# A retention and RWKV-7 decoder trunk: small matmuls in four quarters of the array, a written order table, and the first three projections summed side by side

## The chip, the cores and the metric

The program runs on one core of a Trainium2 chip. The metric is the device time of one execution in microseconds (us), lower is better. A core has five engines that run their own instruction streams: PE (TensorE, matmuls, with its weight loads listed apart as PEld), DVE (VectorE), ACT (ScalarE), POOL (GpSimd) and SP (SyncE, which here only issues DMAs). PE writes its sums into PSUM, which has eight banks; DVE and ACT read them out.

## The reference, cut to what matters

Two residual layers of width 1024 over 1024 tokens, a SwiGLU feed-forward net behind each, and a final norm. Everything that the change touches lies in the mixer of layer 0:

```python
z = h @ w_in                                  # 1024 x 3840
z_ret, z_rwkv = z[..., :4 * RET_WIDTH], z[..., 4 * RET_WIDTH:]
...                                           # 8 retention heads from z_ret
zs = z_rwkv + mu * (token_shift(z_rwkv) - z_rwkv)
rr, kr, vr, wl, al, gl = jnp.split(zs, split_at, axis=-1)
...                                           # decay, a, gate, kk from the low-rank parts
def step(state, inp):                         # 8 RWKV heads of 64, token by token
    r_t, w_t, k_t, v_t, a_t, b_t = inp
    sa = jnp.einsum('bhij,bhj->bhi', state, a_t)
    state = state * w_t[:, :, None, :] + sa[..., None] * b_t[:, :, None, :] + v_t[..., None] * k_t[:, :, None, :]
    return state, jnp.einsum('bhij,bhj->bhi', state, r_t)
...
return jnp.concatenate([ret_out, rwkv_out], axis=-1) @ w_out
```

## The kernel before, in words

Activations are kept transposed, features on the partitions and tokens along the free side, in two halves of 512 tokens (`HT`). A big product is made of float32r matmuls of 128 x 128 weights on 128 x 512 activations; each factor is split into a rounded high part and the rest, so that one product takes three matmuls (high by high, high by low, low by high) and one output tile of 128 features 24 of them. `wsplit` makes the split of a weight tile: a cast on ACT (L339) and a subtraction on DVE or POOL (L340).

The mixer (`mixer0`) has 60 such projections: for each half the two low-rank ones (`lora`), twelve for r, k, v of the RWKV heads and sixteen for the retention heads. They are `jobs` of the class `Plan`. Each sums into one of three PSUM banks of the tag "f" and is then read out by its `evac`, which multiplies by the row factor `self.rs` of the norm (L638 for the RWKV parts, through a single buffer `z`).

Between them stand the small matmuls of the heads, in plain float32, which the profile shows as two records each. They sum into four banks of the tag "m" and one of the tag "c". The RWKV heads go in pairs: partitions 0 to 63 hold one head, 64 to 127 the other. A generator `pair` prepares one pair of one half (eight in all, letters below are tile names):

- n: `BK` by `AR`, 16 matmuls of 64 rows by 64 columns of the array with 64 moving columns; read out by DVE (L726) into `DT` and sent by DMA to `dn`.
- GG: `BK` by `AR`, 64 rows by 128 columns; read out by DVE (L766).
- the transposes of `BK` and of v (`rv`), L258, and the copy of `AR` through an identity into `XA`.
- UV by GG, again 64 by 64, into the other half of `XA`.

A generator `unit` then works on two pairs (four units): it solves a 32 x 32 triangular system on DVE (`X`), fetches it by DMA into `GT`, completes `GT` through two groups of 32 x 32 matmuls (TZ), and runs GT by XA (64 by 64, 128 moving columns), GG by GG (the same shape), and then a chain of eight dependent steps over the chunks (GT, L950 on DVE) that carries the state. `ret` does the retention heads.

In the 64 by 64 groups the two heads of a pair use the array's quarters on the diagonal: rows 0 to 63 with columns 0 to 63, and rows 64 to 127 with columns 64 to 127.

The order is set in two stages. `Plan.run` keeps a clock of its own (`self.now`, advanced by a cost for each matmul) and decides from due times in the `yield`s which generator goes on and when the next third of a projection product is issued. What it emits is then put into each engine's queue by a list scheduler of the framework, which can move instructions a short way past each other.

At the start `loads` fetches the eight x tiles with the first two weight tiles (512 KB each) between them; `first_norm` multiplies x by the norm's gain (ACT L472, DVE L473), squares it (ACT L538) and adds (DVE L540); the sum over the features is a matmul with ones, and `factor` makes `self.rs` from it (L482, L483).

Behind the mixer come the output projection (`wout`, L354 to L356, whose first half is already fed in between the last unit's matmuls), the feed-forward net, the attention layer and its net. They are the same before and after.

Of the kernel before, what the change touches and what calls it, by code (L numbers as in the profile page):

```python
# [16 lines left out]
P = 128  # L17
T = 1024
HT = 512
# [5 lines left out]
CW = math.exp(-0.5)  # L25
NCH = 8
# [75 lines left out]

class Plan:

    def __init__(self, K):
        self.K, self.now, self.ev, self.banks = K, 0.0, {}, []
        self.gens, self.jobs, self.cur, self.twice = [], deque(), None, ()
        self.proj = None  # L110

    def chain(self, g):
        self.gens.append([g, (), self.now])
        return self

    def job(self, name, hf, col, rhs, evac, need=()):
        self.jobs.append(dict(name=name, hf=hf, col=col, rhs=rhs, evac=evac, need=need, raw=None, hl=None))

    def done(self, name):
        self.ev[name] = self.now  # L120

    def time(self, need, t):
        for n, d in need:
            if n not in self.ev:
                return None
            t = max(t, self.ev[n] + d)
        return t

    def rsok(self):
        return self.K.rs is not None  # L130

    def room(self):

        self.banks = [t for t in self.banks if t > self.now]
        return len(self.banks) < 3.0
# [13 lines left out]
    def busy(self):  # L149

        if self.cur is not None:
            return self.cur["k"] < len(self.cur["rhs"])
        if not self.jobs:
            return False
        t = self.time(self.jobs[0]["need"], 0.0)
        return t is not None and t <= self.now

    def step(self):
        c = self.cur
        if c is None:  # L160
            if not self.jobs:
                return None
            t = self.time(self.jobs[0]["need"], 0.0)
            if t is None or t > self.now:
                return t
            self.prefetch()
            c = self.cur = self.jobs.popleft()
            self.prefetch()
            c["ps"], c["k"], c["rhs"] = self.K.pst("f", [P, HT]), 0, c["rhs"]()
        k = c["k"]  # L170
        if k >= len(c["rhs"]):
            return None
        (hi, lo), (rh, rl) = c["hl"][k], c["rhs"][k]
        n = KT
        self.K.mm(c["ps"], hi, rh, start=k == 0, stop=False)
        self.K.mm(c["ps"], hi, rl, start=False, stop=False)
        self.K.mm(c["ps"], lo, rh, start=False, stop=k == n - 1)
        c["k"] += 1
        if c["k"] == n:
            c["evac"](c["ps"])  # L180
            self.done(c["name"])
            self.cur = None
        return self.now

    def run(self):
        while self.gens or self.jobs or self.cur:
            nxt = []
            hold = self.proj is not None and self.busy() and self.rsok() and self.now - self.proj < 0.0
            for g in self.gens:
                t = self.time(g[1], g[2])  # L190
                if not hold and t is not None and t <= self.now and (self.room() or not self.busy()):
                    self.proj = None
                    try:
                        need, d = next(g[0])
                        g[1], g[2] = need, self.now + d
                    except StopIteration:
                        self.gens.remove(g)
                    break
                if t is not None:
                    nxt.append(max(t, self.now + 0.1))  # L200
# [1806 lines left out]
```

## Time and profile before

| what | value |
|---|---|
| three runs | 2315.28, 2315.53, 2315.76 us, median 2315.53 |
| the profiled execution's own time | 2311.46 us |
| its span | 2308.4 us, granted PE clock 0.996 on the mean |
| PE busy | 2260.1 us, 98% of the span |
| DVE busy | 1606.3 us, 70% |
| ACT busy | 1040.5 us, 45% |
| first product matmul | 5.88 us |
| last mixer matmul | about 642 us |

The span is what the profiler saw of one execution; the execution's own time holds 3.06 us more. In the timeline a row stands for a run of like instructions: its start, its length to the end of the last one, how many, and in brackets the idle time of the engine before it. Since matmuls overlap, what a run costs PE is read from its start to the start of the next run, not from its length.

### The profile page before, as it was taken

What the parts mean: (1) busy time and instruction counts of PE and PEld (TensorE: products, weight loads), DVE (VectorE), ACT (ScalarE), POOL (GpSimd) and SP (SyncE); (2) the same over time, 40 slices, a digit from 0 to 9 for tenths busy, and PEclk for the clock granted to TensorE, in tenths of its full rate; (3) what the DMA queues carried; (4) which work ended last, traced back from release to release, by engine and by line L of the source; (5) the groups of instructions that cost most, each with busy time, mean ns of one, the idle gap of its engine ahead of it and who ended that gap; (6) DMA issues with size and microseconds to landing.
All of it is one profiled execution on the core that took longest, in us unless ns stands there. A gap on an engine that the chain in (4) does not pass through costs nothing.

```text
span 2308.4 us, 34970 instructions
## 1 busy us (share of the span) xinstructions
PE 2260.1 (98%) x12980; PEld 1799.4 (78%) x12980; DVE 1606.3 (70%) x2786; ACT 1040.5 (45%) x1962; POOL 432.3 (19%) x439
## 2 busy tenths in 40 slices
PE   8999999999999999999999999999999999999997
PEld 6777777777777888888888877677788888888885
DVE  6876865875567358887677538557448788878778
ACT  5454433414456334444333546456545444443334
POOL 3233221212551000000001743342331000000000
PEclk9999999999999999999999999999999999999998
DMA  8565644443445655663753422242336565647652
GB/s 290 196 226 185 196 145 139 130 126 110 146 174 183 211 176 200 210 215 128 263 215 135 135 84 67 64 137 81 110 132 233 187 215 201 213 179 286 237 203 103
DMA packets 168264, 396.19 MB, mean 172 GB/s; under 512 B 42912, under 2 KB 46112, under 8 KB 168096
## 3 DMA queue, kind: packets, MB, share of 16 engines
q1 hardware_dynamic: 164976, 388.41, 49.8%
q10 hardware_dynamic: 2832, 4.52, 0.5%
q8 instruction: 102, 1.67, 0.3%
q0 software_dynamic: 288, 1.05, 0.1%
q14 instruction: 66, 0.54, 0.1%
HBM read 271.62 MB, written 116.92 MB: 168 GB/s over the span
## 4 chain that ended last, share of the span: by engine, by line
PE 65%; DVE 4%; ACT 2%; issue 1%; DMA 1%; POOL 1%; SPq 0%; ACTq 0%; DVEq 0%; POOLq 0%
PE ps_m L1193 7%; PE ps_m L1192 7%; PE ps_m L1191 7%; PE ps_f L355 4%; PE ps_f L354 4%; PE ps_f L356 4%; PE ps_f L1191 4%; PE ps_f L1192 4%; PE ps_f L1193 4%; PE ps_c L1192 2%; PE ps_c L1193 2%; PE ps_c L1191 2%; PE ps_r L1193 2%; PE ps_r L1192 2%; PE ps_r L1191 2%; PE ps_rc L1674 1%
## 5 line engine op out<-in xcount | busy, mean ns | idle before, releaser
L247 PE MATMUL ps_f<-n,w 128*128 128x512 f32 x1440 | 374.4, 409 | 7.9 <-ACT w L339 5.9
L247 PEld LDWEIGHTS ps_f<-n,w 128*128 128x128 f32 x1440 | 266.8, 190 | 87.5 <-issue 18.6
L340 POOL TENSOR_TENSOR w<-wr,w 128x512 fp32r<-128x512 f32 (+1 forms) x130 | 178.8, 1382 | 383.4 <-ACT w L339 326.4
L339 ACT CAST w<-wr 128x512 fp32r<-128x512 f32 x240 | 145.8, 612 | 167.5 <-PE ps_f L356 65.6
L354 PE MATMUL ps_f<-n,w 128*128 128x512 f32 x356 | 140.6, 396 | 2.4 <-DVE h L603 1.6
L356 PE MATMUL ps_f<-n,w 128*128 128x512 f32 x356 | 140.7, 396 | 1.3 <-POOL w L340 1.3
L355 PE MATMUL ps_f<-n,w 128*128 128x512 f32 x356 | 141.2, 397 | 0.3 <-POOL n L362 0.3
L1191 PE MATMUL ps_f<-n,w 128*128 128x512 f32 x322 | 126.7, 395 | 2.3 <-ACT u L1345 1.6
L1192 PE MATMUL ps_f<-n,w 128*128 128x512 f32 x322 | 125.7, 391 | 0.0
L1193 PE MATMUL ps_f<-n,w 128*128 128x512 f32 x322 | 124.5, 392 | 0.0
L340 DVE TENSOR_TENSOR w<-wr,w 128x512 fp32r<-128x512 f32 x110 | 81.3, 740 | 44.3 <-ACT w L339 44.1
L1191 PE MATMUL ps_m<-n,w 128*128 128x512 f32 x282 | 109.7, 389 | 0.0
L1192 PE MATMUL ps_m<-n,w 128*128 128x512 f32 x282 | 109.7, 389 | 0.0
L1193 PE MATMUL ps_m<-n,w 128*128 128x512 f32 x282 | 109.5, 389 | 0.0
L1191 PE MATMUL ps_m<-cb,w 128*128 128x512 f32 x240 | 93.4, 389 | 0.0
L1192 PE MATMUL ps_m<-cb,w 128*128 128x512 f32 x240 | 93.4, 389 | 0.0
L1193 PE MATMUL ps_m<-cb,w 128*128 128x512 f32 x240 | 93.4, 389 | 0.0
L362 POOL TENSOR_TENSOR ha<-hr,ha 128x512 fp32r<-128x512 f32 x4 | 5.9, 1470 | 447.5 <-ACT ha L360 446.8
L340 DVE TENSOR_TENSOR w<-wq,w 128x512 fp32r<-128x512 f32 x92 | 63.5, 691 | 33.1 <-ACT w L339 32.6
L354 PEld LDWEIGHTS ps_f<-n,w 128*128 128x128 f32 x356 | 66.8, 188 | 19.4 <-issue 2.0
L355 PEld LDWEIGHTS ps_f<-n,w 128*128 128x128 f32 x356 | 66.8, 188 | 18.9 <-issue 4.8
L339 ACT CAST w<-wq 128x512 fp32r<-128x512 f32 x92 | 57.2, 622 | 53.2 <-PE ps_m L1193 29.5
(529 smaller groups left out, 5887.3 us busy)
## 6 DMA issues: line engine op xcount, KB each, us to landing
hc<-n SPq DMA_DIRECT2D x74, 512.0 KB, 3.1
wsp<-w SPq DMA_DIRECT2D x54, 512.0 KB, 3.0
w<-wsp SPq DMA_DIRECT2D x54, 512.0 KB, 3.6
wq<-in_w_gate SPq DMA_DIRECT2D x44, 512.0 KB, 4.1
u<-u SPq DMA_DIRECT2D x88, 256.0 KB, 3.0
n<-hc SPq DMA_DIRECT2D x43, 512.0 KB, 6.4
hid<-n SPq DMA_DIRECT2D x66, 256.0 KB, 2.1
ha<-hc SPq DMA_DIRECT2D x33, 512.0 KB, 5.8
```

The costliest lines, as they stand in the source:

```text
L247: i = self.nc.tensor.matmul(out, lhsT, rhs, **kw)
L339: nc.scalar.copy(hi[:, :n], raw[:, c])
L340: (lo or self.lo).tensor_tensor(out=l[:, :n], in0=raw[:, c], in1=hi.bitcast(F32)[:, :n], op=ALU.subtract)
L354: nc.tensor.matmul(ps, hi, rh, start=k == 0, stop=False)
L355: nc.tensor.matmul(ps, hi, rl, start=False, stop=False)
L356: nc.tensor.matmul(ps, lo, rh, start=False, stop=k == n - 1)
L362: e.tensor_tensor(out=lo, in0=src, in1=hi.bitcast(F32), op=ALU.subtract)
L1191: mm(ps, hi, xh, start=first and k == 0, stop=False, skip_group_check=True)
L1192: mm(ps, hi, xl, start=False, stop=False, skip_group_check=True)
L1193: mm(ps, lo, xh, start=False, stop=last and k == len(w) - 1, skip_group_check=True)
L1674: nc.tensor.matmul(ps[:, e, i, kw], qt[2 * g + i][a, P * b : P * b + P], src[a, P * b + P * k0 : P * b + 256], start=True, stop=True,)
```

## The change

- **Four quarters.** In the 64 by 64 groups (n, the copy of AR, UV by GG, GT by XA, GG by GG) some chunks now use the diagonal quarters as before and the others the two quarters off the diagonal, by the tables `XOF`, `YOF` and `ZOF`. The results of the off-diagonal quarters land on the partitions of the other head, so the order of the heads in `GG`, `XA`, `UV` and `M` changes with the chunk. Matmuls of different rows go to different banks: a group that took one bank takes two, and its read-out becomes two instructions of half the width.
- The transposes of `BK` alternate between the row halves. Those of v are cut in two: 64 rows and 64 moving columns where there were 128 and 128.
- The off-diagonal 32 x 32 blocks that the first TZ group reads now come by DMA through a new buffer `df`: two more writes for each pair and four more reads for each unit.
- **The order table.** `Plan`'s clock and due times are gone. A string `ORDER` says which generator goes on (a letter) and how many products of a projection are issued ahead of it (a number).
- **The start.** The first three projections are summed side by side in the three "f" banks, one feature tile after the other, from weight pieces (`w_first`, 128 x 384, laid out ahead by the host) that land in the places of the `BK` tiles. The next two sum into "m" banks. Six matmuls on a zeroed tile stand ahead of it all.

```diff
+XOF = [c // 2 % 2 for c in range(8)]
+YOF = [c % 2 for c in range(8)]
+ZOF = [c // 2 % 2 ^ c % 2 for c in range(8)]
+XS = (slice(0, 2), slice(2, 4))
+ZS = (slice(0, 4, 3), slice(1, 3))
...
+ORDER = (
+    "aabcdefghijklmnopqrstuv17f13f2g15f3f3g7f4f1f1f4gn2gf3f1f1n1bn3bg1nb1fgg1bg1g3bgng2b3b3b3b1g1b3b2ob3b3b1o1bo3"
...
+        for x in ORDER:
+            if x.isdigit():
+                n += x
+                continue
+            for _ in range(int(n or 0)):
+                self.step()
+            n = ""
+            next(self.gens[ord(x) - ord("a")], None)
...
+        ps = self.t(self.ps, [P, HT], "ps_c", 1)
+        for _ in range(6):
+            nc.tensor.matmul(ps[:, :200], self.idle[:, :P], self.idle, start=True, stop=True)
...
         for k in range(KT):
+            if k % 4 == 0:
+                raw = self.t(self.mz, [P, NCH, 3, 64], "BK", 2).rearrange("p a b c -> p (a b c)")
+            w = raw[:, k % 4 * 3 * P : (k % 4 + 1) * 3 * P]
             x = self.t(rp, [P, HT], "r2", 8)
+            self.keep(nc.sync.dma_start(w, self.A["w_first"][k]))
             self.keep(nc.sync.dma_start(x, self.A["xT"][k, :, 0:HT]))
...
+            j["bank"] = "m"
...
         for k in range(KT):
+            W.append(self.wsplit(wf[k], 3 * P))
+            self.nT.append(self.gained(x0[k], "n1a", n8, k))
...
+            for j, i in ((0, k), (1, k), (2, k - 1)):
+                if i >= 0:
+                    prods(j, i)
...
-        ps = self.pst("m", [P, NCH, 64])
-        for c in range(NCH):
-            for rs in half:
-                self.mm(ps[rs, c, :], BK[rs, c, 0, :], AR[rs, c, 0:64], start=True, stop=True)
+        pss = [self.pst("m", [P, 4, 64]) for _ in range(2)]
+        for c in (0, 2, 1, 3, 4, 6, 5, 7):
+            x = XOF[c]
+            for e, rs in enumerate(half):
+                self.mm(pss[x][half[e ^ x], c // 4 * 2 + c % 2, :], BK[rs, c, 0, :], AR[rs, c, 0:64], start=True, stop=True)
...
+        for q in range(2):
+            nc.sync.dma_start(
+                self.dfs[u][((p % 2) * 2 + q) * 8 : ((p % 2) * 2 + q) * 8 + 8].rearrange("c s t -> s c t"),
+                nd[64 * q : 64 * q + 32, :, 32:64],
+            )
...
-        for e in range(2):
-            ps = self.pst("m", [P, NCH, 64])
-            rs = half[e]
-            for c in range(NCH):
-                self.tr(ps[:, c, :], BK[rs, c, e : e + 2, :].rearrange("p a t -> p (a t)"), ident[rs, rs])
-            S.copy(GG[:, :, e, P:], ps)
+        pss = [self.pst("m", [P, NCH, 64]) for _ in range(2)]
+        for c in range(NCH):
+            for f in range(2):
+                e = f ^ YOF[c]
+                self.tr(pss[f][:, c, :], BK[half[f], c, e : e + 2, :].rearrange("p a t -> p (a t)"), ident[half[f], half[f]])
+        for f in range(2):
+            S.copy(G4[:, :, ZS[f], P:], pairs2(pss[f]))
...
+            for c in range(NCH):
                 for e, a in enumerate(half):
+                    self.mm(pss[ZOF[c]][half[e ^ ZOF[c]], c // 2, :], GT[a, c, :], XA[a, c, :], start=True, stop=True)
+            for f in range(2):
+                for e, a in enumerate(half):
+                    S.copy(four(GG[a, :, e, 0:64])[:, :, ZS[f], :], pairs2(pss[f][a, :, 0:64]))
+                    V.tensor_copy(four(UV[a, :, e, :])[:, :, ZS[f], :], pairs2(pss[f][a, :, 64:P]))
```

How PE's queue changes is seen at three places. In these rows the names are the bank that is summed into, then what streams through and what stands as weights; shape is that of the output. The first place is PE at the start of the program, where `n` and `w` are the split activations and weights. Before, one sum and then a second:

```order
L247 MATMUL ps_f_223<-n_37_166,w_114 128x512
L247 MATMUL ps_f_273<-n_35_164,w_127 128x512
L247 MATMUL ps_f_273<-n_39_168,w_127 128x512
L247 MATMUL ps_f_223<-n_41_170,w_114 128x512
L247 MATMUL ps_f_223<-n_37_166,w_114 128x512 x2
L247 MATMUL ps_f_273<-n_35_164,w_127 128x512 x2
L247 MATMUL ps_f_273<-n_39_168,w_127 128x512
```

And now, at the end of the three sums, with the matmul on ones for the norm and the fourth sum in an "m" bank:

```order
L215 MATMUL ps_f_171<-n_34_165,w_288 128x512
L215 MATMUL ps_f_172<-n_34_165,w_271 128x512
L215 MATMUL ps_f_172<-n_38_169,w_271 128x512
L215 MATMUL ps_f_172<-n_34_165,w_271 128x512
L215 MATMUL ps_m_313<-nq_293,c_ones_68 128x512
L215 MATMUL ps_f_172<-n_34_165,w_288 128x512
L215 MATMUL ps_f_172<-n_38_169,w_288 128x512
L215 MATMUL ps_f_172<-n_34_165,w_288 128x512
L1172 MATMUL ps_m_373<-n_31_162,w_305 128x512
```

The matmul on ones stood behind 59 product matmuls and now stands behind 69, and the sum that follows the first three no longer takes one of their banks. The second place is PE in the first pair of heads, the transposes of `BK`, the copy of `AR` and the transposes of v (`rv`), between products of the projections. Before:

```order
L258 MATMUL ps_m_807<-c_ident_154,BK_530 128x64 x8
L247 MATMUL ps_f_837<-n_39_168,w_732 128x512
L247 MATMUL ps_f_837<-n_35_164,w_732 128x512
L247 MATMUL ps_f_837<-n_36_165,w_732 128x512
L258 MATMUL ps_m_817<-c_ident_154,BK_530 128x64 x8
L247 MATMUL ps_m_842<-c_ident_154,AR_527 64x64 x16
L258 MATMUL ps_m_861<-c_ident_154,rv_424 128x128 x4
L247 MATMUL ps_m_874<-AR_701,BK_704 64x64 x16
L258 MATMUL ps_m_896<-c_ident_154,rv_424 128x128 x4
```

Now the same pair's transposes of `BK`, and further on the next pair's n:

```order
L218 MATMUL ps_m_844<-c_ident_152,BK_546 128x64 x6
L218 MATMUL ps_m_845<-c_ident_152,BK_546 128x64 x6
L218 MATMUL ps_m_844<-c_ident_152,BK_546 128x64
L218 MATMUL ps_m_845<-c_ident_152,BK_546 128x64
...
L215 MATMUL ps_m_876<-AR_724,BK_727 64x64 x2
L215 MATMUL ps_m_877<-AR_724,BK_727 64x64 x2
L215 MATMUL ps_m_876<-AR_724,BK_727 64x64 x2
L215 MATMUL ps_m_877<-AR_724,BK_727 64x64 x2
```

The n group alternates between two banks, that is between the quarters on and off the diagonal, by twos. The transposes do so only in part: the scheduler has put six of one row half ahead of six of the other. The third place is PE in the first unit, GT by XA. Before, four banks one after the other:

```order
L247 MATMUL ps_f_1814<-n_35_164,w_1647 128x512
L247 MATMUL ps_m_1739<-XA_841,GT_1459 64x128 x8
L247 MATMUL ps_m_1752<-XA_841,GT_1459 64x128 x8
L247 MATMUL ps_m_1765<-XA_1130,GT_1460 64x128 x8
L247 MATMUL ps_m_1778<-XA_1130,GT_1460 64x128 x8
```

Now two banks in turn, and then the other two:

```order
L215 MATMUL ps_m_1844<-XA_937,GT_1546 64x128 x2
L215 MATMUL ps_m_1845<-XA_937,GT_1546 64x128 x4
L215 MATMUL ps_m_1844<-XA_937,GT_1546 64x128 x4
L215 MATMUL ps_m_1845<-XA_937,GT_1546 64x128 x4
L215 MATMUL ps_m_1844<-XA_937,GT_1546 64x128 x2
L215 MATMUL ps_m_1870<-XA_1184,GT_1547 64x128 x2
L215 MATMUL ps_m_1871<-XA_1184,GT_1547 64x128 x4
```

The number of matmuls is the same; each bank now holds one set of quarters.

More of the change, by code (lines that the diff above doesn't have):

```diff
@@ L147, in prefetch @@
                     j["hl"] = self.K.wkept(kept) if j["hf"] else self.K.wsplit(j["raw"], keep=kept)
[L149 to L156, printed above, removed]
-    def step(self):
[L159 to L165, printed above, removed]
+    def step(self):
+        if self.cur is None:
             self.prefetch()
@@ L168, in step @@
             self.prefetch()
[L169 removed]
+            c["ps"], c["k"], c["rhs"] = self.K.pst(c.get("bank", "f"), [P, HT]), 0, c["rhs"]()
+        c = self.cur
         k = c["k"]
[L171 to L177, printed above, removed]
+        self.K.prod(c["ps"], [c["hl"][k]], [c["rhs"][k]], k == 0, k == KT - 1)
         c["k"] += 1
[L179 removed]
+        if c["k"] == KT:
             c["evac"](c["ps"])
[L181 removed]
             self.cur = None
[L183 removed]
     def run(self):
[L186 to L200, printed above, removed]
[L201 to L208 removed]
+        n = ""
[5 more added lines that the diff above has]
+                self.step()
+            n = ""
+            next(self.gens[ord(x) - ord("a")], None)
+        for _ in range(int(n or 0)):
+            self.step()
+        assert not self.jobs and self.cur is None
 class Kern:
@@ L297, in pst @@
     def pst(self, tag, shape):
-        if tag == "m" and self.plan:
-            self.plan.banks.append(self.plan.now + 3.0)
         return self.t(self.ps, shape, "ps_" + tag, self.psb[tag])
@@ new lines, in pair @@
+        for f in range(2):
+            S.copy(G4[:, :, ZS[f], P:], pairs2(pss[f]))
+        yield
+        XA = self.t(mp, [P, NCH, P], "XA", 2)
+        pss = [self.pst("m", [P, 4, 64]) for _ in range(2)]
+        for c in (0, 2, 1, 3, 4, 6, 5, 7):
+            x = XOF[c]
+            for e, rs in enumerate(half):
+                self.mm(
+                    pss[x][half[e ^ x], c // 4 * 2 + c % 2, :], AR[rs, c, 0:64], ident[rs, rs], start=True, stop=True
+                )
+        for f in range(2):
+            S.copy(four(XA)[:, :, XS[f], 0:64], pairs2(pss[f]))
@@ L814, in pair @@
-            yield (), 1.0
-        yield (), 7.5
-        ps = self.pst("m", [P, NCH, 64])
+                    out=UVw[half[i], js, two, e, :], in0=ps[half[i], ji, :],
+                    in1=mean[half[i], ji].to_broadcast([64, js.stop - js.start, 64]), op=ALU.add,
+                )
+            yield
+        yield
+        pss = [self.pst("m", [P, 4, 64]) for _ in range(2)]
         for c in range(NCH):
```

294 lines of the change are left out of this document (128 added, 166 removed).

## Prediction, made before the changed kernel was run

> **What bounds the kernel now.** I read the page's table of engines first, then the windows by stage, then PE's timeline inside them.
>
> ```profile
> PE 2260.1 (98%) x12980; PEld 1799.4 (78%) x12980; DVE 1606.3 (70%) x2786; ACT 1040.5 (45%) x1962; POOL 432.3 (19%) x439
> ...
> 0.00:28.07 28.07, 21.17 (x74) 14.96 (x75) 16.44 (x29) 20.15 (x32) 3.56 (x17) 1.00 0.87 281
> 28.07:577.70 549.63, 535.99 (x4864) 413.30 (x4865) 389.33 (x820) 227.84 (x361) 148.74 (x208) 0.99 0.53 169
> 577.70:652.30 74.60, 70.56 (x646) 55.92 (x645) 41.87 (x76) 37.25 (x62) 37.23 (x29) 1.00 0.39 129
> 652.30:2308.40 1656.10, 1632.36 (x7399) 1315.25 (x7397) 1158.70 (x1864) 755.24 (x1507) 242.78 (x187) 1.00 0.50 173
> ```
>
> In a window row stand the bounds, the length, the busy time (and count) of PE, PEld, DVE, ACT and POOL, then the granted clock, the DMA share and GB/s. PE is busy for 536.0 of 549.6 us in the body of the mixer and for 1632.4 of 1656.1 us behind it. So only three things can change the time: what PE's own instructions cost, the 13.6 us in which PE is idle in 28.07:577.70 (and 4.0 in the next row), and the start, with 21.2 busy of 28.1. The last 1656.1 us hold none of the edited work, and I carry them over.
>
> **The start.** PE's timeline and two windows of it (length, busy time, count):
>
> ```profile
> 5.88 17.37 PE L247 MATMUL ps_f<-n,w 128*128 128x512 f32 x59 [5.88 <-ACT w L339]
> 23.09 1.02 PE L247 MATMUL ps_m<-nq,c_ones 128*128 128x512 f32 x2
> 23.55 3.55 PE L247 MATMUL ps_f<-n,w 128*128 128x512 f32 x13
> 28.07 5.73 PE L247 MATMUL ps_f<-n,w 128*128 128x512 f32 x24 [0.97 <-DVE z L638]
> ...
> 5.88:11.95 6.07, 6.01 (x13) 1.00 0.95 336
> 11.95:23.09 11.14, 11.14 (x48) 1.00 0.89 274
> ```
>
> From start to start, 48 matmuls take 11.14 us, .232 each, but the first 13 take 6.07, .467 each, at a granted clock of 1.00: a matmul costs twice as much in the first microseconds of work. The first three sums (72 matmuls) end at 28.07, with .97 us of waiting for the single buffer `z`. Now 72 matmuls run without that wait, behind six matmuls on zeros that take the dear first microseconds while PE would wait for data. Still 72 x .232 = 16.7, ones .46 (23.09 to 23.55), a first product at the same 5.88 (one weight piece and one x tile, as before), and about 1 us for the part of the dear time that the six do not cover: 24.0 instead of 28.1, a gain of 4.0 us. Bounds: 0 (the interleaved order needs all three weight pieces and an x tile before each further step, so data may take the wait's place; the DMA share of .87 is high) and 5.5 (nothing dear left). I take 4.0, nearer the upper end, because in 11.95:23.09 PE never waited for data. `rs` then comes while the next two sums, in "m" banks, give PE 48 x .232 = 11.1 us of work.
>
> **The small matmuls.** The timeline of PE in the first pairs and the first unit:
>
> ```profile
> 63.75 1.15 PE L247 MATMUL ps_m<-AR,BK 64*64 64x64 f32 x32
> 64.83 0.50 PE L247 MATMUL ps_f<-n,w 128*128 128x512 f32 x1
> ...
> 82.40 0.71 PE L258 MATMUL ps_m<-c_ident,BK 64*128 64x64 f32 x8 [0.37 <-DVE GG L766]
> 83.04 0.98 PE L247 MATMUL ps_f<-n,w 128*128 128x512 f32 x3
> 83.95 0.71 PE L258 MATMUL ps_m<-c_ident,BK 64*128 64x64 f32 x8
> 84.59 1.15 PE L247 MATMUL ps_m<-c_ident,AR 64*64 64x64 f32 x32
> ...
> 162.32 3.71 PE L247 MATMUL ps_m<-XA,GT 64*64 64x128 f32 x64
> 165.97 6.43 PE L247 MATMUL ps_f<-n,w 128*128 128x512 f32 x27
> 173.29 1.50 PE L247 MATMUL ps_m<-UV,GG 128*64 128x64 f32 x32 [0.90 <-DVE UV L913]
> 174.72 1.96 PE L247 MATMUL ps_m<-GG 64*64 64x128 f32 x32
> 176.61 1.15 PE L247 MATMUL ps_m<-UV,GG 128*64 128x64 f32 x32
> ...
> 178.94 1.09 PE L247 MATMUL ps_m<-GG 64*64 64x128 f32 x16 [1.18 <-DVE XA L924]
> ...
> 576.07 1.09 PE L258 MATMUL ps_m<-c_ident,r 128*128 128x128 f32 x8
> 576.92 0.95 PE L247 MATMUL ps_f<-n,w 128*128 128x512 f32 x3
> ```
>
> A float32 matmul is two records. From start to start, 64 records of 128 moving columns take 3.65 us (162.32 to 165.97) and 32 take 1.89 (174.72 to 176.61): .055 a record and .13 for the group. Thirty-two of 64 columns take 1.08 (63.75 to 64.83): (1.08 - .13) / 32 = .030. Two matmuls, in the diagonal quarters, run at once there: a transpose of 64 columns that fills half the rows costs .64 / 8 = .08, or about .061 without what the change of shape costs, twice .030. So with four at once a group's records cost half. That four do run at once, the trace shows where two groups happen to meet, r by Sc in the diagonal quarters and UV by GG in the others:
>
> ```profile
> 562.11 0.27 PE L247 MATMUL ps_m<-UV,GG 64*64 64x64 f32 x2
> 562.21 0.28 PE L247 MATMUL ps_m<-r,Sc 64*64 64x128 f32 x2
> 562.22 0.28 PE L247 MATMUL ps_m<-UV,GG 64*64 64x64 f32 x4
> 562.32 0.28 PE L247 MATMUL ps_m<-r,Sc 64*64 64x128 f32 x2
> ...
> 562.11:562.43 0.32, 0.32 (x21) 1.00 1.02 422
> 63.86:64.68 0.82, 0.82 (x31) 1.00 0.85 195
> ```
>
> The two windows give 21 records in .32 us, .015 each, against 31 in .82, .026 each, though a part of the 21 has 128 columns. Halving is therefore the price I take; the other bound is no gain.
>
> A group gains only where the order on PE really alternates. I counted that, group by group, in the changed order:
>
> - n: 8 of 8 pairs, 16 record times of .030 = .47 each: 3.8.
> - the copy of AR and UV by GG: about 6.5 of 8 each, .47: 3.1 and 3.1.
> - GT by XA: 7/8 of four units, 32 x .055 = 1.76 each: 6.1.
> - GG by GG: .9 of eight groups, 16 x .055 = .87 each: 6.3.
> - transposes of `BK`: 4.5 of 8 pairs, 8 x .061 = .49 each: 2.2.
> - transposes of v: now eight of .106 (576.07 to 576.92, eight in .85); then eight of .061 as halves, one after the other in four pairs (.36 less each) and by twos in four (.61 less): 3.9.
>
> Sum 28.5 us. Bounds: 2.9, if only the shorter stream for v counts (8 x .36), and 34, if every group alternates.
>
> **What the new order costs PE.** It changes the array's shape (full, half, quarter) 306 times up to the last mixer matmul, against 268: 38 more, 19 round trips. One trip is priced by 83.04 to 83.95: three products take .91 where 3 x .23 = .69 is their due, .22 at the way out; and .64 for eight transposes is .15 more than 8 x .061, for the way in. Together .37, and 19 x .37 = 7.0 us lost. Bounds: 0, because some of the extra changes stand inside groups of small matmuls that overlap anyway (at 562.11 none is seen), and 9.
>
> [...]
>
> **Work beside PE.** The read-outs are the same elements in more, smaller pieces, and SP gets 32 more DMAs:
>
> ```profile
> 178.20 0.68 DVE L924 TENSOR_TENSOR XA<-ps_m,PC 128x512 f32<-128x512 f32 x1
> 180.02 0.42 DVE L934 TENSOR_TENSOR XA<-ps_m,c_id 128x256 f32<-128x256 f32 x1
> 182.61 0.68 DVE L726 TENSOR_TENSOR DT<-ps_m,c_gmask 128x512 f32<-128x512 f32 x1
> ...
> 67.32 2.09 SPq L733 DMA_DIRECT2D dn<-DT  x4
> ...
> dn<-DT SPq DMA_DIRECT2D x32, 32.0 KB, 1.6
> GT<-dg SPq DMA_DIRECT2D x32, 32.0 KB, 2.3
> ```
>
> A half-width read costs .42 instead of .68, so .16 more for each read cut in two. Some 50 such cuts are 8 us of DVE and ACT, under DVE's 389.3 busy of 549.6; without that cover they would be 8 us. Each extra DMA is half a microsecond of issue (2.09 for four, 16 us in all) and about 2 us to land. SP's queue holds only issues, and the new ones follow the writes of the same `dn` block; they serve the first TZ group, which until now waited for GG besides. What is queued behind them on SP are the reads for `X` of the same pair, late by the new issues' 2 to 3 us at the most; the solve on DVE would wait for that. I cost both at nothing, between -6 (the order spreads the stalls, since TZ is freed) and +8. PE's waits that remain, by who ends them (us, times, mean us):
>
> ```profile
> PE ps_m L247 <- DVE GT L950: 2.2, 2, 1.2
> PE ps_c L247 <- DVE GT L950: 2.0, 1, 2.0
> PE ps_m L247 <- DVE XA L924: 1.2, 1, 1.2
> PE ps_m L247 <- DVE UV L913: 1.1, 2, 0.9
> PE ps_m L247 <- DVE AR L938: 0.9, 1, 0.9
> ```
>
> They are few and short, each a place where a small product waits for the read-out of the last; the table rewrites the order around all of them, and I leave their sum as it is.
>
> **The sum.** 28.5 + 4.0 - 7.0 = 25.5 us less than the profiled execution's 2311.46: 2286.0. The median of the runs lies 4.07 above that execution, so 2290 for the median, 1.1% faster.
>
> **The rivals.**
>
> *A: the read-out sets the pace.* Where PE waits for what a small group has made (173.29, 178.94), a group that ends sooner only waits longer, since DVE's reading starts bank by bank and takes .42 to .68 a piece. GT by XA and GG by GG feed the chain of the units, which has just those waits; if their 12.4 us come back as idle time, the time is 2290 + 12.4 = 2302. For it: all five rows above end on DVE. Against it: most groups are followed by products of the projections (64.83, 165.97), which do not wait. [...] In this trace DVE is at 71% in the stage, which neither bears it out nor excludes it for the units.
>
> *B: quarters on and off the diagonal still go two by two.* The case of 562.11 might be special, since two groups there have different weights on other rows. Then remain v and half of `BK` (3.9 + 2.2), the start's 4.0, and the 7.0 lost: 3 us, 2312, within what can be told from no change.
>
> *C: slower, from want of "m" banks.* There are four; n, the copy, UV by GG, GT by XA and GG by GG now take two at a time, at 8 places each, 40 in all. If each then waits as the two places above do for a bank's read-out (.90 and 1.18), that is about 36 us, and 2290 + 36 = 2326. It decides from 25.5 / 40 = .64 us a place. For it: a bank is free only after its read-out, and both halves now end together. Against it: groups are spaced by products (27 behind 165.97), and two half reads take .84, the time of four products.
>
> **How the numbers follow.** Forecast .68, A .15, B .07, C .10. The forecast's own range is 2278 (no loss at the changes, and all groups overlap) to 2300 (start 0 and stalls +6). The range of 8 in 10, 2275 to 2306, adds A and stalls that shrink by 3 more; it leaves out B and C. A measurement of this kernel can hardly tell .2% (4.6 us) from no change; by that bound faster holds the forecast and A, .83, the same holds B, .07, and slower holds C, .10.
>
> **What would show it.** After: the fourth sum's first matmul at about 24 us and no wait for `z` ahead of it; n in about .6 us for 32 records (1.08 now); GT by XA in 1.9 for 64 (3.65 now); GG in .6 for 16; body and tail of the mixer about 21 us shorter together; PE's idle time there near 18 us; the last 1656 us unchanged. I am wrong if 32 records of n still take 1 us (B), if rows of PE with "m" tiles show new waits behind DVE L924 and its neighbours (A) or ahead of groups that wait for a bank (C), or if the work behind the mixer moves.

## The result: slower, by 0.6%

| | before | changed |
|---|---|---|
| median of five runs | 2315.53 us | 2329.31 us (2322.69 to 2333.89) |
| ratio | | 1.0058, interval 1.0044 to 1.0071 |
| profiled execution's span | 2308.4 us | 2332.1 us |
| granted PE clock, mean of the span | 0.996 | 0.982 |

The forecast was 2290 us, range 2275 to 2306. The profiled execution of the changed kernel is the slowest of its five (the other four had a mean clock of .986 or .987, by which the clock takes some 9 us less from them), so what follows explains 23.7 us of span, 14 of which are in the medians.

First the windows, of both kernels, from 26 us to a matmul of the feed-forward net that stands 19 us behind the net's first in both, and from there to the end. The columns are length, busy time and count of PE, PEld, DVE, ACT, POOL, granted clock, DMA share, GB/s. Before:

```profile
26.00:718.78 692.78, 671.23 (x5788) 520.73 (x5786) 472.19 (x944) 304.13 (x486) 219.59 (x259) 1.00 0.51 167
718.78:2308.40 1589.62, 1568.78 (x7124) 1264.31 (x7124) 1118.53 (x1817) 717.99 (x1448) 209.81 (x165) 1.00 0.50 172
```

Changed:

```profile
26.00:740.49 714.49, 675.28 (x5781) 513.61 (x5779) 467.03 (x951) 307.03 (x504) 219.49 (x259) 0.95 0.50 161
740.49:2332.10 1591.61, 1569.54 (x7124) 1264.48 (x7124) 1117.69 (x1817) 717.63 (x1448) 208.80 (x165) 1.00 0.50 172
```

Behind the mixer nothing moved (1589.6 and 1591.6 us). In the first stretch, the mixer and the output projection above all, PE is idle for 39.2 us where it was idle for 21.5, and its clock is granted at 0.95. That PE is busy 4 us longer hides what the packing did, which PE's timeline of the changed kernel shows:

```profile
61.04 0.69 PE L215 MATMUL ps_m<-AR,BK 64*64 64x64 f32 x32
61.66 0.50 PE L1172 MATMUL ps_f<-n,w 128*128 128x512 f32 x1
...
175.12 1.98 PE L215 MATMUL ps_m<-XA,GT 64*64 64x128 f32 x64
177.03 0.50 PE L1172 MATMUL ps_f<-n,w 128*128 128x512 f32 x1
...
194.65 1.10 PE L215 MATMUL ps_m<-GG 64*64 64x128 f32 x32
195.68 1.15 PE L215 MATMUL ps_m<-UV,GG 128*64 128x64 f32 x32
```

n takes .62 us (1.08 before), GT by XA 1.91 (3.65), GG by GG 1.03 for 32 records (1.89). Four quarters do run at once: the three groups take .52 to .57 of the time they took before.

The clock is the new thing. In these windows of the changed kernel PE does almost nothing for one stretch, and has half its clock for the next two:

```profile
181.36:184.77 3.41, 0.23 (x4) 0.22 (x4) 2.70 (x7) 2.53 (x7) 0.78 (x3) 1.00 0.84 318
184.77:191.59 6.82, 6.62 (x43) 4.28 (x40) 5.79 (x11) 3.36 (x8) 1.82 (x3) 0.50 0.43 151
191.59:195.00 3.41, 3.41 (x53) 2.68 (x55) 0.93 (x2) 1.47 (x3) 1.35 (x2) 1.00 0.83 192
```

All changes of the clock in this trace lie on one grid of 3.413 us (82.37, 92.61, 119.91, 123.33, 184.77, 191.59 and so on). I call such a stretch at half clock a spell. The first stretch of the changed kernel has 20 of them, that of the kernel before 2, at 425.4 and 500.5.

With that, the stretch from 26 us on splits into three parts that sum up to its length. PE's work is its busy time, counted half where the clock is one half (products of 512 columns start .43 us apart there, at 82.54 to 83.82, and .23 before); the clock's loss is the other half. Both are worked out from all PE records of the trace.

| us | PE's work at full clock | idle | lost by the clock | sum |
|---|---|---|---|---|
| before | 667.8 | 21.5 | 3.4 (2 spells) | 692.8 |
| changed | 644.2 | 39.2 | 31.0 (20 spells) | 714.5 |
| difference | -23.6 | +17.7 | +27.6 | +21.7 |

PE's waits of the changed kernel in that stretch (us in total, times, longest):

```profile
PE ps_f L311 <- DVE h L576: 5.2, 2, 4.7
PE ps_m L215 <- DVE bv L730: 4.3, 2, 2.6
PE ps_m L215 <- DVE UV L895: 4.2, 2, 4.0
PE ps_m L215 <- DVE XA L906: 3.6, 1, 3.6
PE ps_m L215 <- DVE GT L933: 3.2, 2, 3.0
PE ps_c L215 <- DVE GT L933: 2.9, 1, 2.9
PE ps_m L215 <- DVE GG L748: 2.7, 3, 1.8
PE ps_m L218 <- DVE GG L748: 2.5, 2, 1.6
```

They end as often as before on DVE, but the longest is 4.7 us instead of 2.0. In most of them the waiting matmuls do not read what DVE wrote: n of a later pair waits until `UV` has been read out (4.0 us at 184.54), the transposes of `BK` until GG has. So they seem to wait for a bank. The longest, 4.7 us, stands in the output projection, behind the mixer.

### The profile page after: what moved, and what is told of

Same layout as the page of the kernel before. It is cut to its first block, busy times and chain, and to the rows that moved or that the text cites. A ratio compares the mean times of both kernels' runs of the same rounds, so it can differ in the third digit from the quotient of the medians.

```text
span 2332.1 us, 35072 instructions
## 1 busy us (share of the span) xinstructions
PE 2269.6 (97%) x12992; PEld 1797.9 (77%) x12992; DVE 1600.9 (69%) x2796; ACT 1042.0 (45%) x1980; POOL 431.2 (18%) x439
## 4 chain that ended last, share of the span: by engine, by line
PE 79%; DVE 9%; ACT 4%; DMA 4%; issue 3%; SPq 1%; POOL 1%; ACTq 0%; DVEq 0%; POOLq 0%
PE ps_m L1174 7%; PE ps_m L1173 7%; PE ps_m L1172 7%; PE ps_f L1172 6%; PE ps_f L1173 6%; PE ps_f L1174 6%; PE ps_f L312 5%; PE ps_f L311 5%; PE ps_f L313 5%; PE ps_m L215 4%; PE ps_c L1174 2%; PE ps_c L1173 2%; PE ps_c L1172 2%; PE ps_r L1174 2%; PE ps_r L1173 2%
## 5 line engine op out<-in xcount | busy, mean ns | idle before, releaser
L1172 PE MATMUL ps_f<-n,w 128*128 128x512 f32 x750 | 310.7, 414 | 4.7 <-DMA w<-wsp 2.4
L1173 PE MATMUL ps_f<-n,w 128*128 128x512 f32 x750 | 304.1, 406 | 0.0
L1174 PE MATMUL ps_f<-n,w 128*128 128x512 f32 x750 | 302.9, 405 | 0.0
L1172 PEld LDWEIGHTS ps_f<-n,w 128*128 128x128 f32 x750 | 143.9, 192 | 47.1 <-issue 14.1
L1173 PEld LDWEIGHTS ps_f<-n,w 128*128 128x128 f32 x750 | 144.1, 192 | 37.4 <-issue 8.3
L1174 PEld LDWEIGHTS ps_f<-n,w 128*128 128x128 f32 x750 | 143.9, 192 | 37.3 <-issue 6.3
L311 PE MATMUL ps_f<-n,w 128*128 128x512 f32 x356 | 142.2, 400 | 5.9 <-DVE h L576 5.2
L312 PE MATMUL ps_f<-n,w 128*128 128x512 f32 x356 | 142.5, 400 | 0.0
L313 PE MATMUL ps_f<-n,w 128*128 128x512 f32 x356 | 140.5, 395 | 0.0
L1172 PE MATMUL ps_m<-n,w 128*128 128x512 f32 x300 | 116.7, 389 | 0.0
L1173 PE MATMUL ps_m<-n,w 128*128 128x512 f32 x300 | 116.7, 389 | 0.0
L1174 PE MATMUL ps_m<-n,w 128*128 128x512 f32 x300 | 116.5, 389 | 0.0
L1172 PE MATMUL ps_m<-cb,w 128*128 128x512 f32 x236 | 91.8, 389 | 0.0
L1173 PE MATMUL ps_m<-cb,w 128*128 128x512 f32 x236 | 91.8, 389 | 0.0
L1174 PE MATMUL ps_m<-cb,w 128*128 128x512 f32 x236 | 91.8, 389 | 0.0
L297 DVE TENSOR_TENSOR w<-wq,w 128x512 fp32r<-128x512 f32 x91 | 63.0, 692 | 34.8 <-ACT w L296 34.4
L311 PEld LDWEIGHTS ps_f<-n,w 128*128 128x128 f32 x356 | 67.4, 189 | 23.5 <-issue 6.8
L312 PEld LDWEIGHTS ps_f<-n,w 128*128 128x128 f32 x356 | 67.4, 189 | 18.2 <-issue 4.6
```

Of the source, the lines that this page charges most:

```text
L297: (lo or self.lo).tensor_tensor(out=l[:, :n], in0=raw[:, c], in1=hi.bitcast(F32)[:, :n], op=ALU.subtract)
L311: nc.tensor.matmul(ps, hi, rh, start=k == 0, stop=False)
L312: nc.tensor.matmul(ps, hi, rl, start=False, stop=False)
L313: nc.tensor.matmul(ps, lo, rh, start=False, stop=k == n - 1)
L1172: mm(ps, hi, xh, start=first and k == 0, stop=False, skip_group_check=True)
L1173: mm(ps, hi, xl, start=False, stop=False, skip_group_check=True)
```

## The experiments

Every median is of runs beside the kernel before on the same chip, whose medians there were 2313 to 2316 us; where runs beside different medians are compared, the ratios say more than the times. The last three columns are the split of the profiled execution, as above.

| run | median | ratio (interval) | work | idle | clock |
|---|---|---|---|---|---|
| e1 changed, old order | 2330.0 | 1.0067 (1.0045-1.0088) | 648.1 | 42.5 | 22.0 |
| e2 changed, long filler | 2349.9 | 1.0150 (1.0131-1.0170) | 698.2 | 25.2 | 10.1 |
| e3 changed, two quarters | 2333.5 | 1.0083 (1.0065-1.0101) | 665.5 | 31.5 | 17.6 |
| e4 changed, products moved | 2331.8 | 1.0071 (1.0049-1.0093) | 646.0 | 45.4 | 18.5 |
| e5 changed, five "m" banks | 2341.1 | 1.0107 (1.0090-1.0124) | 642.9 | 49.8 | 27.4 |
| e6 old order, two quarters | 2340.9 | 1.0107 (1.0092-1.0122) | 671.2 | 35.7 | 14.3 |
| e7 before, new start | 2314.7 | 0.9992 (0.9980-1.0005) | 661.8 | 26.3 | 8.2 |
| e8 changed, short filler | 2339.0 | 1.0101 (1.0080-1.0122) | 666.6 | 38.0 | 13.2 |
| e9 changed, no extra transfers | 2326.3 | 1.0052 (1.0037-1.0067) | 648.3 | 40.4 | 18.6 |
| e10 old order, no extra transfers | 2318.3 | 1.0023 (1.0012-1.0035) | 651.1 | 34.8 | 12.0 |
| e11 before, extra transfers | 2319.5 | 1.0027 (1.0017-1.0037) | 668.1 | 26.6 | 6.2 |
| e12 extra transfers on ACT's queue | 2325.1 | 1.0048 (1.0031-1.0066) | 649.4 | 35.9 | 21.7 |
| e13 before, two banks everywhere | 2359.0 | 1.0195 (1.0178-1.0212) | 677.1 | 41.6 | 20.8 |
| e14 before, 105 matmuls fewer | 2308.8 | 0.9975 (0.9964-0.9985) | 646.1 | 27.6 | 16.2 |
| e15 before, two banks for three groups | 2342.8 | 1.0125 (1.0106-1.0143) | 673.8 | 34.1 | 13.9 |
| e16 before, BK transposes in turn | 2316.2 | 1.0015 (1.0006-1.0025) | 666.8 | 25.0 | 3.2 |
| e17 as e15, order kept | 2326.0 | 1.0054 (1.0034-1.0075) | 673.3 | 23.7 | 10.1 |
| e18 before, only the reads in two | 2315.4 | 1.0001 (0.9991-1.0010) | 667.1 | 21.1 | 6.2 |

### Does the order, or the packing, bring the low clock? (e1 to e4)

e1 takes the sequence of steps that the planner of the kernel before found, and writes it as the table:

```diff
-ORDER = ("aabcdefghijklmnopqrstuv17f13f2g15f3f3g7f4f1f1f4gn2g...")
+ORDER = ("abcdefghijklmnopqrstuva17f13f11g6f1f4g6f4f1f1f1f1gf1gn2f6bng2...")
```

> The changed kernel with the order that the planner of the kernel before had found, written as a table (two calls of each unit, which the change has merged into others, are left out). Theory 1: the changed table leaves PE idle before groups that wait for a bank, and each idle patch takes the granted clock to one half for one or two spells of 3.41 us; the old order spaces the groups by products. Then idle time and half-clock spells fall back to near those of the kernel before (about 20 us and 2 to 6 spells, against 39 us and 20 now), and the time is 2290 to 2305 us. Theory 2: it is the groups that take two banks and all four quarters at once, whatever the order, that bring the waits or the low clock. Then there are still 14 spells or more and the time is 2318 us or more.

2330.0 us: the old order is no better. By its own words this speaks for theory 2, but only for its second half: the groups with two banks bring the waits.

e2 puts matmuls on zeros ahead of twelve groups:

```diff
+            if x == "*":
...
+                self.K.mm(self.cur["ps"], self.K.idle[:, :P], self.cur["rhs"][0][0].bitcast(F32), start=False, stop=False, skip_group_check=True)
```

> The changed kernel with 61 matmuls on zeros (weights of zeros, added into the projection sum under way, so that they change nothing) put ahead of the twelve groups before which PE now idles longest. They do no useful work and add none. Theory 1 (idle time lowers the clock): PE's idle time falls by about 20 us and is replaced by these matmuls, the half-clock spells fall from 20 to 6 or fewer, and although nothing else is saved the time falls to 2296 to 2310 us. Theory 2 (the dense use of the four quarters lowers the clock): the spells stay at 14 or more and the time is 2325 to 2345 us.

The spells fell from 20 to 6, with all four quarters in use as before (n takes .63 us). So the packing by itself does not lower the clock here, and theory 2 falls there: with the waits filled, the clock takes 10.1 us where it took 31.0. The time did not follow, because each filler took .89 us, 54 us in all, not 27.

e3 sets the five groups back on two quarters:

```diff
-                self.mm(pss[x][half[e ^ x], c // 4 * 2 + c % 2, :], BK[rs, c, 0, :], AR[rs, c, 0:64], start=True, stop=True)
+                self.mm(pss[x][half[e], c // 4 * 2 + c % 2, :], BK[rs, c, 0, :], AR[rs, c, 0:64], start=True, stop=True)
```

> The changed kernel with the five 64 by 64 groups back on two quarters (the same banks, places and order; the heads in the results are then mixed up, so the output is not the reference's, but every instruction is there). Theory 1: PE's own work grows by about 22 us at full clock (3.8 + 3.1 + 3.1 + 6.1 + 6.3), the longer groups take up some of the idle time, half-clock spells stay at 10 or more, and the time is 2335 to 2352 us. Theory 2: with no four quarters at once the spells fall to 4 or fewer, and the time is 2312 to 2325 us.

PE's work grew by 21.3 us, as expected (22), and the median by 4.2 (5.8 by the ratios). In the profiled executions eight of the 21 came out of idle time and 13 out of the clock's loss. This is the first sign that PE's work is not what sets the time here.

e4 moves 31 products ahead of nine of the waits (in the table, `1f` becomes `5f`, `bbbh` becomes `bbb6h`, and so on):

> The changed kernel with 31 products of the projections moved ahead of nine of the groups before which PE idles (taken one each from the places that follow). Theory 1: idle time in the mixer falls by 8 us or more, half-clock spells to 12 or fewer, time 2295 to 2318 us, since products cover the read-out that frees a bank. Rival: VectorE is late whatever PE does, and the waits only move on to the places from which the products were taken: idle time within 5 us of now, 15 spells or more, 2322 us or more.

The time stayed (2331.8): the rival's time, with idle time even higher (45.4), though the spells fell to 13. Other waits took the places of those that were filled, the longest at 688.03 with 6.5 us.

### Is it the number of banks, the lengths, the start, the low clock? (e5 to e8)

```diff
-        pq = self.psum("ps0", {"f": 3, "m": 4, "c": 1})
+        pq = self.psum("ps0", {"f": 2, "m": 5, "c": 1})
```

> The changed kernel with five PSUM banks for the small groups and two for the projections (the third of the first three sums goes into one of the five). Most of PE's new waits end with VectorE reading out some other tile, that is with a bank coming free. Theory 1a (want of banks makes the waits): PE's idle time in the mixer falls from 39 to 30 us or less, the half-clock spells from 20 to 12 or fewer, and the time is 2300 to 2318 us. Theory 1b (VectorE, ScalarE and the transfers behind them are late in themselves, and more banks let PE run ahead only to the next wait): idle time within 5 us of now and the time 2322 us or more.

Worse, 2341.1. The fifth bank was taken from the projections, and what they lost by it cannot be told apart here, so this run decides nothing on theory 1a.

e6 is e1 with the edit of e3:

> The changed kernel with the order of the kernel before and with the five 64 by 64 groups on two quarters as before (heads mixed up in the results). What is left of the change: the start, two banks for a group with read-outs of half width, and the extra transfers. If it was the order, worked out for other lengths of the groups, that makes the waits: 2310 to 2320 us, 6 spells or fewer. If the two banks and the split read-outs make them: 2326 us or more, 10 spells or more.

2340.9 us, in an order and with quarters like those before. So the loss is in what the two kernels still differ in: start, banks, read-outs, transfers. Against e1 it also gives the quarters another price: 11 us (9 by the ratios), in the old order.

e7 puts the new `loads` and `first_norm`, the six matmuls on zeros and the banks of the next two sums into the kernel before.

> The kernel before with the changed start alone (three sums side by side, the next two in other banks, six matmuls on zeros). If the 2.6 us by which the first three sums end earlier are passed on: 2311 to 2314 us. If the work of the other engines sets when the first small groups can start, PE only comes to them earlier, waits, and pays with a spell or two at half clock: 2315 to 2325 us.

No change, 0.9992. The trace shows where the gain ends. PE is 4.1 us ahead of the kernel before until 77 us, and then:

```profile
80.17 0.85 PE L259 MATMUL ps_m<-c_ident,BK 64*128 64x64 f32 x8 [1.89 <-DVE GG L787]
...
77.16:80.57 3.41, 1.52 (x11) 1.00 0.73 283
80.57:87.40 6.83, 6.83 (x68) 0.50 0.58 186
```

The wait of 1.89 us (.37 in the kernel before, 82.40) takes over a third of the lead, and two spells behind it, 3.41 us, more than the rest. At 88.9 us PE is .7 us behind.

e8 is e2 with 42 fillers of 256 columns, sized to the waits:

> As the run with matmuls on zeros, whose 61 matmuls took some 54 us of PE's time in place of the 27 us that were meant, but with 42 of half the length, sized to the waits (about 19 us). If idle time alone lowers the clock: idle time falls by 12 us or more, the spells from 20 to 8 or fewer, and the time to 2302 to 2318 us, with nothing useful done by the added work. If spells follow from something else: 2328 us or more.

A miss in an instructive way. The spells fell to 9 and the clock's loss by 17.8 us, but the idle time stayed (38.0) and the filler's 22 us came on top:

```profile
26.00:743.90 717.90, 679.89 (x5858) 0.98 0.51 160
```

It seems that PE at full clock only came to its waits earlier. What the filler gave it took, so it does not show what a cure without cost would be worth.

### The extra transfers (e9 to e12)

SP's queue and DVE's waits show them. First SP before, around the second pair's n:

```profile
88.79 1.81 SPq L733 DMA_DIRECT2D dn<-DT  x4
...
91.88 1.12 SPq L837 DMA_DIRECT2D DT<-dn  x2
```

and changed:

```profile
92.69 1.81 SPq L709 DMA_DIRECT2D dn<-DT  x4
94.54 0.94 SPq L714 DMA_DIRECT2D df<-DT  x2
96.25 0.30 SPq L848 DMA_DIRECT2D GT<-df  x1
...
97.23 1.14 SPq L815 DMA_DIRECT2D DT<-dn  x2
```

At this place the DT reads are issued 4.54 us behind the dn writes, where it was 3.09. DVE waits for them; its waits for transfers before (total, times, longest):

```profile
DVE xt L848 <- DMA DT<-dn: 8.2, 3, 4.6
DVE TZ L875 <- DMA GT<-dg: 6.2, 4, 3.4
```

and changed:

```profile
DVE xt L826 <- DMA DT<-dn: 14.1, 4, 5.2
DVE TZ L858 <- DMA GT<-dg: 9.2, 9, 2.6
```

(The text sent ahead of e9 says that there was no wait for dg before; there was, 6.2 us.) e9 and e10 leave the transfers out of the changed kernel and of e1, e11 adds them to the kernel before, e12 issues them from ACT's queue. The edit of e9, with its calls shortened:

```diff
-        for q in range(2):
-            nc.sync.dma_start(self.dfs[u][...], nd[64 * q : 64 * q + 32, :, 32:64])
...
-        for q in range(4):
-            nc.sync.dma_start(GTs[q // 2][r0 : r0 + 32, :, 32:64], df[...])
```

> The changed kernel without its 32 extra transfers (the first TZ group then reads zeros, so the output is not the reference's). In the runs so far VectorE, which works in order, waits longer for transfers than before: 14.1 us for DT from dn and 9.2 us for TZ from dg in the changed kernel, 8.2 and none before. Theory 3: the extra writes stand on SP between the dn writes and the DT reads, and hold the DT tile; VectorE's solve comes late, every read-out behind it too, and PE's waits and half-clock spells follow. Then VectorE's waits for transfers fall by 8 us or more, and the time is 2300 to 2318 us. Theory 4 (two banks for a group, read-outs in halves): within 5 us of the changed kernel, 2324 to 2334 us.

> The changed kernel with the order of the kernel before and without the 32 extra transfers (first TZ group on zeros). Theory 3: 2295 to 2315 us, since the order then meets the delays it was worked out for, and PE's shorter groups count. Theory 4: 2322 us or more.

> The kernel before with the 32 extra transfers alone; what they bring is not used and is overwritten. Theory 3: the DT reads come 1.5 to 3 us later in each unit, PE waits, some spells at half clock follow: 2321 to 2340 us. Theory 4: 2313 to 2318 us, no change.

> The changed kernel with the 32 extra transfers issued by ScalarE's queue in place of SP's. If it is their place on SP ahead of the DT reads that costs (theory 3, issue of half a microsecond each): 2312 to 2323 us. If it is that the DT tile cannot be refilled before the writes from it have landed, or that the transfers themselves crowd others: 2324 us or more. Theory 4: 2324 to 2334 us.

Alone in the kernel before they cost 6.4 us (2319.5 against 2313.1), outside every range written for it: less than theory 3 said and more than theory 4. Taking them out gives back 3.0 in the changed order (1.4 by the ratios), not more than its runs scatter, and 11.8 in the old one (10 by the ratios), again between the two theories. On ACT's queue the changed kernel takes 2325.1 us, which these runs cannot tell from the 2326.3 without the transfers, nor surely from the 2329.3 with them on SP's. So the transfers are a part of the loss, and most of the rest is elsewhere.

### Two banks in turn, and whether PE is the bound (e13 to e18)

e15 changes n, the copy of AR and UV by GG in the kernel before, as here; e13 does the like to GT by XA, GG by GG and the transposes of `BK` too:

```diff
-        ps = self.pst("m", [P, NCH, 64])
+        pss = [self.pst("m", [P, 4, 64]) for _ in range(2)]
...
-                self.mm(ps[rs, c, :], BK[rs, c, 0, :], AR[rs, c, 0:64], start=True, stop=True)
+                self.mm(pss[c % 2][rs, c // 2, :], BK[rs, c, 0, :], AR[rs, c, 0:64], start=True, stop=True)
```

> The kernel before with the changed use of banks alone: n, the copy of AR, UV by GG, GT by XA, GG by GG and the transposes of BK fill two banks in turn and are read out in two pieces at their end, on the same two quarters as before, with the planner of before. Theory 5: this is where the missing 19 us are, since both banks are ready only at the group's end and four banks hold no more than two groups: 2326 to 2340 us. Theory 6 (the loss needs the shorter groups, the table or the transfers): 2310 to 2319 us.

> The kernel before with two banks in turn and read-outs in halves for n, the copy of AR and UV by GG alone. Theory 5: part of the loss, 2318 to 2330 us, by how much of it these three groups carry. Theory 6: 2313 to 2319 us.

Both lose much more than expected, but not for one reason: the planner counts banks, counted two for each of these groups, and chose quite another order. e17 lets it count such a pair once, and keeps nine tenths of PE's order in place (the edit against e15):

```diff
-        pss = [self.pst("m", [P, 4, 64]) for _ in range(2)]
+        pss = [self.pst("m", [P, 4, 64]), self.t(self.ps, [P, 4, 64], "ps_m", self.psb["m"])]
```

> The kernel before with two banks in turn and read-outs in halves for n, the copy of AR and UV by GG, and a planner that counts such a pair of banks once, so that its order is (but for single steps of the list scheduler) that of the kernel before. Theory 5 (the use of banks is the loss, in whatever order): 2322 to 2340 us. Theory 9 (the loss was the order that the planner chose for it): 2312 to 2320 us.

2326.0 us, 1.0054: theory 5. At 24 places (three groups, eight pairs) a second bank costs 11 us (8 to 17 by the interval), about .46 a place, with no quarter, order table, start or transfer changed. It does not all come as waits: against the kernel before the split shows 5.5 us more of PE's work, 2.2 of idle time and 6.7 lost by the clock. Of the 5.5 the three groups themselves take 1.4, and the rest is spread over the others; what the tenth of the order that did move has to do with it is open. e18 keeps the one bank and only reads it in two pieces:

```diff
+        pss = [ps[:, 0:4, :], ps[:, 4:8, :]]
```

> The kernel before with the results of the same three groups read out in two pieces of half the width, out of one bank as before. A half-width read costs .42 us in place of .34, so about 4 us more on VectorE and ScalarE in all. If the pieces are the loss: 2318 us or more. If it is the second bank: 2312 to 2317 us.

No change, 1.0001: the loss comes with the second bank, not with the pieces. e16 only lets the transposes of `BK` take turns between the row halves, into two banks:

> The kernel before with only the transposes of BK taking turns between the row halves (two banks at once, read-outs as they were). PE's work falls by up to 3.9 us (8 x 8 x .061). If PE is the bound: 2310 to 2313 us. If the second bank costs what the overlap saves: 2314 to 2322 us.

2316.2: here, too, the second bank costs a little more than PE's work falls (1.0 us).

e14 is the test of the premise:

```diff
+        if self.left % 4 == 3 and k:
+            self.now += 0.000443 * 512
+        else:
+            self.K.mm(c["ps"], hi, rl, start=False, stop=False)
```

> The kernel before without the second of three matmuls in 105 products of the projections (every fourth sum), 24 us of PE's time, with the planner's clock kept as it was, so that the order stays (the sums are then less exact). Theory 7: PE is the bound of the mixer, time saved there is saved: 2289 to 2296 us. Theory 8: the chain over VectorE, ScalarE and the transfers stands right behind PE; most comes back as idle time and half-clock spells: 2303 us or more.

```profile
26.00:715.90 689.90, 662.34 (x5690) 0.98 0.51 167
```

2308.8 us. Taking 24 us of products out of the kernel before, with no other edit, makes it 5.7 us faster. In the split PE's work is 21.8 us less, the idle time 6.0 more and the clock's loss 12.8 more. No run beats the kernel before while doing its work; e7 and e18 equal it.

## Why the prediction was wrong, step by step

**The packing (28.5 us).** Right. Taken group by group, from start to start without idle time and at full clock, the seven groups fell from 72.9 to 47.3 us, by 25.6: n 3.1 (forecast 3.8), the copy 2.4 (3.1), UV by GG 3.4 (3.1), GT by XA 5.7 (6.1), GG by GG 5.9 (6.3), `BK` 2.2 (2.2), v 2.9 (3.9). Rival B falls with that.

**Changes of shape (7.0 us lost).** Half as much, on the net: all other PE work of the stretch grew by 3.6 us, worked out as the seven groups' 25.6, less the 23.6 by which the whole fell, and 1.6 for seven products that now lie ahead of 26 us. This is a sum in which other differences hide. In e15, with 37 more changes of shape and no group shortened, PE's work grew by 6.0 us, so it is not settled that the price read from the rows was too high.

**The start (4.0 us).** Right in size, though not in this trace, and then lost. The row of the last of the three sums before ended at 28.07; it is now

```profile
1.07 4.37 PE L395 MATMUL ps_c<-pad 128*128 128x200 f32 x12 [1.07 <-POOL zlast L373]
5.60 18.50 PE L215 MATMUL ps_f<-n,w 128*128 128x512 f32 x69 [0.16 <-ACT n L432]
23.93 1.02 PE L215 MATMUL ps_m<-nq,c_ones 128*128 128x512 f32 x2
24.39 1.26 PE L215 MATMUL ps_f<-n,w 128*128 128x512 f32 x3
```

and the fourth sum starts at 25.48: 2.6 us. In this execution the full clock came at 10.69, 5 us into the products, which start .43 us apart until then and .23 behind. In the eleven other traces with this start it came between 4.49 and 6.71, and the fourth sum started between 23.53 and 24.85, near the forecast of 24.0. This is e7's:

```profile
5.74 0.49 PE L248 MATMUL ps_f<-n,w 128*128 128x512 f32 x1 [0.30 <-ACT n L476]
6.53 16.14 PE L248 MATMUL ps_f<-n,w 128*128 128x512 f32 x68 [0.29 <-DVE n L477]
...
24.05 1.32 PE L248 MATMUL ps_m<-n,w 128*128 128x512 f32 x5
```

In the eight traces with the old start, the full clock came between 10.34 and 13.67 us. So the six matmuls on zeros, with which PE starts at 1.07 instead of 5.88, seem to do what they were meant to do, but for the one trace of the changed kernel. e7 shows that none of the gain reaches the end.

**"I cost both at nothing", with stalls between -6 and +8, and "I leave their sum as it is" on PE's waits.** This is the step that failed. The idle time rose by 17.7 us. Of the two costs put at nothing, the read-outs in pieces are so (e18), but the extra transfers cost 6.4 us alone in the kernel before (e11). The prediction's sentence on SP named the harm, a solve on DVE that waits 2 to 3 us longer, and then priced it at nothing. And the second bank, which has no term in the sum and stands in rival C alone, costs 11 us at 24 places (e17).

**The clock was left out of the sum.** The trace of before showed it: half clock from 425.42 on, right behind a stretch in which PE idles for almost half the time.

```profile
422.01:425.42 3.41, 1.86 (x42) 1.19 (x38) 3.38 (x11) 0.00 (x0) 1.31 (x2) 1.00 0.43 147
425.42:428.83 3.41, 3.41 (x16) 1.69 (x17) 3.27 (x11) 1.78 (x4) 0.36 (x2) 0.50 0.00 0
```

The argument spoke of dear microseconds at the start alone. So every wait was priced at its length. In the changed kernel all ten waits of 1.6 us or more were followed by one to three spells, of up to 1.7 us loss each; in the kernel before, one of 2.0 was (498.74) and one of 1.6 was not (620.96). In the window above, 1.55 us of idle time out of 3.41 was enough; in the changed kernel's window from 474.90 to 478.31 it was 1.12.

**The premise: with PE at 98%, a microsecond of PE is a microsecond of time.** e14 refutes it for the kernel before: of 24 us, 5.7 arrive. A share of 98% tells that PE is seldom idle. It does not tell how far the others are behind it. In the mixer they stand right behind: of what PE gained in e14, 6.0 us came back as idle time and 12.8 as lost clock, and DVE ends 23.7 of the 27.6 us that PE idles there.

**The rivals.** C gave 2326 us by want of "m" banks, with the point of decision at .64 us a place. The time is near, and so is the price: .46 a place at the 24 places that e17 changes, though of the 14 us by which that stretch grew there only 2.2 are idle time. That C comes so near is in part luck: it had 36 us of waiting alone, and the runs show 17.7 us of idle time, 27.6 lost by the clock and a cost of the transfers. In the sum of single costs, 11 for three of the groups' banks and 6.4 for the transfers stand against 4 (e3) to 11 us (e6 against e1) that the quarters bring; that leaves 6 to 13 us slower, beside the 13.8 measured. That the costs may be added so is not shown. e6, with all but the table and the quarters, is 26 us above before, so 8 or 9 us of it stay open: the second bank of GT by XA, GG by GG and the transposes, or their calls that now follow each other without products between. A says in part what happened, that DVE sets the pace, at 2302 too small a price.

**What stays open** beside that: how much of the clock's 27.6 us would be gained if it stayed up. The fillers (e2, e8) brought it back and cost as much themselves.

## What to carry to other kernels

A high busy share (98% here) does not make an engine the bound: take work out of it and see (e14 took out 24 us, and 5.7 arrived), before working out what faster work is worth. Price what packing needs, not only what it saves: a second accumulation bank for a group, held to the group's end, cost .46 us a place here, more than the .37 of PE's time that the packing saved at those places on the mean (n, the copy and UV by GG, 8.9 us over 24). And price a wait on the matmul engine with what it may do to the clock, up to three times its length for one of some 1.8 us here (422.41 in the changed kernel: 1.84 us, and 3.41 lost in the two spells from 423.70 on).

## What the runs showed of the hardware that I had not expected

In the changed kernel up to 740 us the clock went to one half eleven times, each time right behind a window of 3.41 us in which PE idled for 1.1 to 3.2 us; it stayed there for one window (three times), two (seven) or three (once), and its changes lie on the grid of 3.413 us. Counted over the windows at full clock in all twenty traces, half clock followed on none of those with less than .5 us of idle time, on 18 of 401 with .5 to 1.5, on 39 of 65 with 1.5 to 2, and on all 67 with 2 us or more. Idle time is not the whole measure. These are windows of the changed kernel:

```profile
116.50:119.91 3.41, 1.83 (x23) 1.00 0.41 113
253.04:256.45 3.41, 2.27 (x18) 1.00 0.01 2
256.45:263.27 6.82, 6.22 (x13) 0.50 0.68 218
737.73:741.14 3.41, 1.82 (x9) 1.00 0.17 25
741.14:744.56 3.42, 3.42 (x17) 1.00 0.94 277
```

The first and the fourth are busy for the same time; behind the first, 23 records with small matmuls among them, comes half clock at 119.91; behind the fourth, nine of the big ones, the clock stays. The second, with 1.14 us idle, is followed by two spells. What decides beside the idle time is not shown.
